# Holding back the first segment's expert gathers until the second segment's front has ended

## The chip, the core and the metric

The kernel runs on one core of a Trainium2 chip. The metric is the device time of one execution in microseconds (us). A core has five engines with an instruction queue each, worked off in order: TensorE (PE, with its weight loads listed apart as PEld), VectorE (DVE), ScalarE (ACT), GpSimd (POOL) and SyncE (SP, which here issues the plain DMAs). Engines wait for each other through semaphores. DMAs run beside the engines; indirect DMAs (gathers, one row of DRAM for each partition) are issued by POOL.

## The reference, cut to what matters

One layer: a mixer (four mLSTM heads and eight heads of forgetting attention), an output projection, and then a PEER channel mixer, which retrieves 8 x 16 experts out of 16384 for every token.

```python
def block(xb):                                   # 128 tokens
    qh = (xb @ w_query).reshape(tb, PEER_HEADS, 2, PEER_HALF)
    scores = einsum('thpc,hpnc->thpn', qh, keys)
    val, idx = top_k(scores, 16)                 # for each half of the key
    cand = val[..., 0, :, None] + val[..., 1, None, :]
    top_s, pos = top_k(cand.reshape(tb, 8, 256), 16)
    ids = take_along_axis(cand_id, pos)          # (tb, 128) experts per token
    gate = softmax(top_s)
    act = gelu(einsum('ted,td->te', u_emb[ids], xb))
    return einsum('te,ted->td', gate * act, v_emb[ids])
```

There are 1024 tokens of width 1024 (and 16 meta tokens before them); a row of `u_emb` or `v_emb` has 1024 float32 numbers.

## The kernel before, in words

The 1024 tokens are cut into four segments of two blocks of 128 (`SEGS`). Each segment goes through a front: `proj` (norm, projections, gates), `mlstm`, `fox` (attention) and `outp` (output projection, second norm, and at its end, line 854, the transposes of the normed tokens, 16 per segment). The loop over `i` near the end of the program merges the front of segment `i` with `proj` of segment `i + 1`, and with `topk`, the choice of experts: that of segment 0 is merged into `i = 1`, that of segments 1 and 2 into `i = 3`. Weights are split for the matmuls into a high part `wh` (cast on ACT, line 277) and a low part `wl` (subtraction on DVE, line 282, or on POOL, line 280).

The experts are computed in two ways. Segments 1 and 2 take the dense way: `gates` builds a table of gate weights for all 16384 experts (matmuls `gout`, line 1136, from one-hot tiles that DVE, ACT and POOL, line 1134, write), and the dense loop at the end of the program multiplies with all of `peer_u` (matmuls `du`, line 289) and all of `peer_v` (matmuls `vo`, line 1222), 1920 and 3072 of them.

Segments 0 and 3 take the gathered way, `gather_rows`. For a block A or B of 128 tokens there are 128 gathers of `peer_u` (line 325: retrieved expert r of every token, 128 rows of 4 KB, so 0.524 MB), each followed by its use: a product with the tokens, summed along the row, on DVE (line 334, 11 of 16) or on POOL with the sum on ACT (lines 331 and 332, 5 of 16). Then 128 gathers of `peer_v` (line 361: all experts of one token); four of these make a group for eight matmuls `po` (line 383). `gather_items` yields all u of block A, then in turn four v of A and four u of B, then all v of B. A use of v stands behind all uses of u of its block.

The gathers of segment 0 are written in the program after `topk` of the last segment (`GP0 = 5`), through a pool of four tiles (`GATH`); a scheduler that runs a timeline of its own at build time sorts each engine's instructions and puts the gathers, which come last and so have the lowest priority, where it sees an engine free from the moment the indices exist. The gathers of segment 3 are `Paced`: each waits for a matmul of the dense loop, 1.08 gathers for a beat, with twelve tiles (`GATH2`); they stand behind those of segment 0 in POOL's queue. The order of each engine is fixed at build time.

Of the kernel before, what the change touches and what calls it, by code (L numbers as in the profile page):

```python
# [19 lines left out]
P = 128  # L20
# [71 lines left out]
def _block_kernel(ctx, tc, nc, I, out, dbg):  # L92
# [27 lines left out]
    def bank(name):  # L120
        turn_b[0] += 1
        if extra is not None and turn_b[0] % XB == 0:
            return extra[:, turn_b[0] // XB % 2, :]
        return ps.tile([P, 512], F32, tag="bank", name=name, bufs=2)
# [9 lines left out]
    dve, act, pe, pool_e, sync = nc.vector, nc.scalar, nc.tensor, nc.gpsimd, nc.sync  # L134
# [6 lines left out]
    ident = identr.bitcast(F32)  # L141
# [67 lines left out]
    def rsqrt(o, x, scale, t):  # L209

        act.activation(o, x, AF.Ln, bias=epsc[0:x.shape[0]], scale=scale)
        act.activation(o, o, AF.Exp, scale=-0.5)
        act.activation(t, o, AF.Square)
        dve.scalar_tensor_tensor(t, x, EPS / scale, t, op0=OP.add, op1=OP.mult)
        dve.tensor_scalar(t, t, -0.5 * scale, 1.5, op0=OP.mult, op1=OP.add)
        dve.tensor_mul(o, o, t)
# [32 lines left out]
    def rawt(name):  # L249
        return wp.tile([P, L], F32, tag="raw", name=name, bufs=RAW)  # L250
# [5 lines left out]
    for i in range(3):  # L256
        c = slice(i * 512, min(L, i * 512 + 512))
        for e, t in enumerate((oz, zo)):
            t = t[0:NH_F, 0:c.stop - c.start]
# [134 lines left out]
    def gather_items(S, share, gp):  # L394

        A, B = (gather_rows(gp, S, lb, share) for lb in range(NB))
        yield from A.u
        for i in range(0, P, 4):
            yield from A.v[i:i + 4]
            yield from B.u[i:i + 4]  # L400
        yield from B.v


    def segment(sg):
        S = SimpleNamespace()
        S.sg = sg
        S.idT = None
        S.nb = nb = SEGS[sg]
        S.xb0 = xb0 = sum(SEGS[:sg])
        S.off = off = NMETA if sg == 0 else 0  # L410
        S.nx = nb * P
        S.n = S.nx + off
        S.c0 = 0 if sg == 0 else NMETA + xb0 * P
        S.chunks = ([(0, NMETA)] if sg == 0 else []) + [(off + i * P, P) for i in range(nb)]
        S.hx = len(S.chunks) - nb
        S.xs = slice(xb0 * P, xb0 * P + S.nx)
        S.T1 = S.c0 + S.n
        return S

    def tok_proj(wsrc, xh, xl, tbs, consume):  # L420

        bks = [acc_bank("tk") for _ in tbs]
        for kp in range(4):
            if xl is None:
                raw = rawt("raw")[:, 0:1024]
                sync.dma_start(raw, wsrc[kp])
                for k in (2 * kp, 2 * kp + 1):
                    for b, (ti, (s0, w)) in zip(bks, tbs):
                        pe.matmul(b[0:w, :], xh[:, k, s0:s0 + w], raw[:, k % 2 * 512:(k % 2 + 1) * 512],
                                  start=(k == 0), stop=(k == KT - 1))  # L430
                continue
            for kk, (h, l) in enumerate(halves(wsrc[kp], 2, share=SHARE)):
                k = 2 * kp + kk
                for b, (ti, (s0, w)) in zip(bks, tbs):
                    a, c = xh[:, k, s0:s0 + w], xl[:, k, s0:s0 + w]
                    for i, (x, wx) in enumerate(((a, h), (a, l), (c, h))):
                        pe.matmul(b[0:w, :], x, wx, start=(k == 0 and i == 0), stop=(k == KT - 1 and i == 2))
        for b, (ti, (s0, w)) in zip(bks, tbs):
            consume(ti, w, b)
# [376 lines left out]
    def outp(S):  # L816

        nb, xb0, yh, yl = S.nb, S.xb0, S.yh, S.yl
        if dbg: dbg("yh", S.sg, yh); dbg("yl", S.sg, yl)
        h2p = sp.tile([P, NB, D], F32, tag="u0", name="h2b")  # L820
        h2s = [h2p[:, b, :] for b in range(nb)]
        for b in range(nb):
            sync.dma_start(h2s[b], I["x"][(xb0 + b) * P:(xb0 + b + 1) * P, :])
        for nq in range(2):
            def take_w(ti, w, b):
                o = h2s[ti][:, nq * 512:(nq + 1) * 512]
                dve.tensor_add(o, o, b)
            tok_proj(I["wo"][nq], yh, yl, [(b, (b * P, P)) for b in range(nb)], take_w)
            yield
        gffn = rawt("gffn")[:, 0:D]  # L830
        sync.dma_start(gffn, I["g_ffn"].partition_broadcast(P))
        if S.sg <= DENSE[1]:
            half_ = slice((S.sg - DENSE[0]) % 2 * NX, ((S.sg - DENSE[0]) % 2 + 1) * NX)
            xh, xl = Xh[:, :, half_], Xl[:, :, half_]
        else:
            xh = hp.tile([P, KT, NTOK], F32R, tag="hh", name="xh3")[:, :, 0:nb * P]
            xl = hp.tile([P, KT, NTOK], F32R, tag="hl", name="xl3")[:, :, 0:nb * P]
        if S.sg in Q32:
            xh, xl = xh.bitcast(F32), None
        S.xh, S.xl = xh, xl  # L840
        for b in range(nb):
            gb_ = xb0 + b
            sync.dma_start(h2d[gb_ * P:(gb_ + 1) * P, :], h2s[b])
            xn = rawt("xn")[:, 0:D]
            ssq = sp.tile([P, 3], F32, tag="ssq", name="ssq")
            act.activation(xn, h2s[b], AF.Square, accum_out=ssq[:, 0:1])
            rsqrt(ssq[:, 1:2], ssq[:, 0:1], 1.0 / D, ssq[:, 2:3])
            dve.scalar_tensor_tensor(xn, h2s[b], ssq[:, 1:2], gffn, op0=OP.mult, op1=OP.mult)
            if S.sg not in DENSE:
                sync.dma_start(xnd[gb_ * P:(gb_ + 1) * P, :], xn)  # L850
            for half in range(2):
                tb = bank("xT")
                for i in range(4):
                    pe.transpose(tb[:, i * P:(i + 1) * P], xn[:, (4 * half + i) * P:(4 * half + i + 1) * P], ident)
                dsth = xh[:, 4 * half:4 * half + 4, b * P:(b + 1) * P]
                if xl is not None:
                    dstl = xl[:, 4 * half:4 * half + 4, b * P:(b + 1) * P]
                tbv = tb.rearrange("p (k t) -> p k t", k=4)
                act.copy(dsth, tbv)
                if xl is not None:  # L860
                    dve.tensor_sub(dstl, tbv, dsth.bitcast(F32))
        yield
# [111 lines left out]
    segs = [segment(i) for i in range(len(SEGS))]  # L974
    NPROJ, NTOP = 2 + 1 + 8 + 2 + 8, NH_P

    def main(S):
        yield from fox(S)
        yield from outp(S)
# [19 lines left out]
            yield  # L999

    def gather(S, share, gp):
        for ask, use in gather_items(S, share, gp):
            use(ask()[0])

    class Paced:

# [18 lines left out]
        def use(self):  # L1025
            _, f, t = self.open.pop(0)
            with ExitStack() as es:
                for k in ("pe", "dve"):
                    if k in seen:
                        es.enter_context(tc.issue_after(seen[k].ins))  # L1030
                f(t)
# [11 lines left out]
    def gather_first(at):  # L1043
        if GP0 == at:
            gather(segs[0], GS0, gp)


    for i in range(-1, len(SEGS)):
# [9 lines left out]
        if i >= 0:  # L1058
            S = segs[i]
# [227 lines left out]
```

## Time and profile before

| | |
|---|---|
| median of 3 runs | 3746.05 us (3735.21 to 3759.56) |
| profiled execution | 3742.05 us, span 3740.3 us |
| PE / DVE / POOL / ACT busy | 81% / 69% / 52% / 38% of the span |
| granted TensorE clock, mean | 0.890 of full speed |
| HBM read, written | 860.91 MB, 67.47 MB |

"Busy" counts an engine's instructions without waits. A wait is told as "idle before, and what ended it". The granted clock is a share of full speed, 1.0 being 2.4 GHz and 0.5 being 1.2 GHz. Each `po` matmul stands in the trace as two records (2048 for 1024).

### The profile page before, as it was taken

To read this page: it belongs to the slowest core of one execution; us is meant where nothing else is said; L and a number is where in the kernel's file an instruction comes from. 1 tells how busy PE (TensorE), PEld (TensorE's weight loads), DVE (VectorE), ACT (ScalarE), POOL (GpSimd) and SP (SyncE) were. 2 spreads that over 40 slices of the span, in tenths; PEclk is the share of its full clock that TensorE was granted. 3 is DMA by queue.
4 is the path that set the end of the run, shared out by engine and by line. 5 is a ranking of instruction groups with operands and counts; after the bars stand their busy time and mean duration, and the time that the engine had idled before them with its cause. 6 is when DMAs were issued, how large, how long until landed. Compare 5 with 4: busy or idle time off the path is not lost. (4 is left out here: it accounts for less than half of the span.)

```text
span 3740.3 us, 47105 instructions
## 1 busy us (share of the span) xinstructions
PE 3040.7 (81%) x15233; PEld 2324.6 (62%) x15233; DVE 2581.1 (69%) x6272; ACT 1435.7 (38%) x2915; POOL 1944.4 (52%) x1575
## 2 busy tenths in 40 slices
PE   7798776657778889887886599865798888989999
PEld 6686666446556667656765476644576555666667
DVE  6566999987447988888997443877655656654434
ACT  4565443345343323335655432322333332332222
POOL 3121566666545545557656422888655555543430
PEclk9899876768788999988998899887899999999999
DMA  4455577777877778767776777988888788889983
GB/s 140 123 156 166 191 228 243 240 226 250 229 241 238 242 223 257 240 239 263 271 251 234 272 253 248 325 285 287 283 295 293 269 284 290 313 317 328 330 292 109
DMA packets 375899, 931.54 MB, mean 249 GB/s; under 512 B 59316, under 2 KB 145556, under 8 KB 373604
## 3 DMA queue, kind: packets, MB, share of 16 engines
q0 software_dynamic: 161216, 552.56, 44.3%
q1 hardware_dynamic: 214436, 375.97, 30.4%
q8 instruction: 120, 1.97, 0.2%
q14 instruction: 127, 1.04, 0.1%
HBM read 860.91 MB, written 67.47 MB: 248 GB/s over the span
## 5 line engine op out<-in xcount | busy, mean ns | idle before, releaser
L282 DVE TENSOR_TENSOR wl<-raw,wh 128x512 fp32r<-128x512 f32 x736 | 608.4, 833 | 508.6 <-ACT wh L277 455.7
L277 ACT CAST wh<-raw 128x512 fp32r<-128x512 f32 x896 | 543.0, 617 | 971.4 <-DMA raw<-in_peer_v 208.5
L325 POOL DMA_INDIRECT gu<-in_peer_u,idx x512 | 578.9, 1131 | 567.9 <-PE po L383 173.7
L361 POOL DMA_INDIRECT gv<-in_peer_v,idT x512 | 558.2, 1090 | 603.4 <-PE po L383 198.2
L334 DVE SCALAR_TENSOR_TENSOR gu<-gu,xng 128x1024 f32<-128x1024 f32 x352 | 512.8, 1467 | 99.0 <-DMA gu<-in_peer_u,idx 91.9
L1222 PE MATMUL vo<-wh,Wh 128*128 128x512 f32 x1024 | 395.1, 418 | 138.5 <-ACT wh L277 114.0
L1222 PE MATMUL vo<-wl,Wh 128*128 128x512 f32 x1024 | 423.1, 413 | 12.2 <-DVE wl L282 12.1
L331 POOL TENSOR_TENSOR gu<-gu,xng 128x1024 f32<-128x1024 f32 x160 | 389.7, 2436 | 71.8 <-DMA gu<-in_peer_u,idx 66.3
L1222 PE MATMUL vo<-wh,Wl 128*128 128x512 f32 x1024 | 415.8, 408 | 0.0
L280 POOL TENSOR_TENSOR wl<-raw,wh 128x512 fp32r<-128x512 f32 x160 | 217.8, 1361 | 325.9 <-ACT wh L277 294.7
L1222 PEld LDWEIGHTS vo<-wh,Wh 128*128 128x128 f32 x1024 | 198.4, 197 | 231.9 <-ACT wh L277 136.3
L383 PE MATMUL po<-gv,Z 128*32 128x512 f32 x2048 | 273.4, 641 | 78.0 <-DMA gv<-in_peer_v,idT 78.0
L332 ACT ACTIVATE gu<-gu 128x1024 f32<-128x1024 f32 x160 | 169.2, 1058 | 364.6 <-POOL gu L331 357.2
L289 PE MATMUL du<-xh,wh 128*128 128x512 f32 x640 | 259.0, 405 | 30.3 <-ACT wh L277 30.3
L289 PE MATMUL du<-xh,wl 128*128 128x512 f32 x640 | 258.8, 405 | 22.2 <-DVE wl L282 22.1
L289 PE MATMUL du<-xl,wh 128*128 128x512 f32 x640 | 256.2, 400 | 0.0
L1222 PEld LDWEIGHTS vo<-wl,Wh 128*128 128x128 f32 x1024 | 204.0, 199 | 69.9 <-DVE wl L282 19.8
L1222 PEld LDWEIGHTS vo<-wh,Wl 128*128 128x128 f32 x1024 | 203.3, 199 | 51.9 <-issue 6.7
L1136 PE MATMUL gout<-A,B 128*128 128x128 f32 x1024 | 161.3, 310 | 65.1 <-POOL B L1134 51.9
L1136 PEld LDWEIGHTS gout<-A,B 128*128 128x128 f32 x1024 | 146.6, 217 | 93.8 <-POOL B L1134 69.9
L1227 DVE TENSOR_TENSOR acc<-acc,vo 128x512 f32<-128x512 f32 x256 | 164.7, 680 | 47.2 <-PE vo L1222 46.7
L1207 DVE TENSOR_TENSOR Wl<-w,Wh 128x512 fp32r<-128x512 f32 x128 | 96.0, 754 | 133.2 <-ACT Wh L1206 113.5
(431 smaller groups left out, 6696.3 us busy)
## 6 DMA issues: line engine op xcount, KB each, us to landing
raw<-in_ut SPq DMA_DIRECT2D x128, 512.0 KB
raw<-in_peer_v SPq DMA_DIRECT2D x256, 256.0 KB
raw<-in_wf SPq DMA_DIRECT2D x64, 512.0 KB
gd<-G SPq DMA_DIRECT2D x16, 2048.0 KB
Gt<-gd SPq DMA_DIRECT2D x32, 1024.0 KB
raw<-in_wt SPq DMA_DIRECT2D x48, 512.0 KB
raw<-in_wq SPq DMA_DIRECT2D x48, 512.0 KB
raw<-in_wo SPq DMA_DIRECT2D x32, 512.0 KB
```

The lines of the kernel that those rows point to most:

```text
L277: act.copy(h, part)
L280: pool_e.tensor_sub(l, part, h.bitcast(F32))
L282: seen["dve"] = dve.tensor_sub(l, part, h.bitcast(F32))
L289: seen["pe"] = pe.matmul(o, w, x[:, c], start=(first and i == 0), stop=(last and i == 2))
L325: d = pool_e.indirect_dma_start(out=t, out_offset=None, in_=I["peer_u"], in_offset=bass.IndirectOffsetOnAxis(ap=S.idx[:, lb, r:r + 1], axi ...
L331: pool_e.tensor_tensor(t, t, xn[0], op=OP.mult)
L332: act.activation(t, t, AF.Copy, accum_out=G.actv[:, r:r + 1])
L334: dve.scalar_tensor_tensor(t, t, 1.0, xn[0], op0=OP.mult, op1=OP.mult, accum_out=G.actv[:, r:r + 1])
L361: d = pool_e.indirect_dma_start(out=t, out_offset=None, in_=I["peer_v"], in_offset=bass.IndirectOffsetOnAxis(ap=S.idT[lb][:, tok:tok + 1], ...
L383: last = pe.matmul(G.po[32 * q_:32 * q_ + 32, n, :], z[:, q_, 31 - j:63 - j], rows[q_][:, n * 512:(n + 1) * 512], start=(j == 0), stop=(j ...
L1136: pe.matmul(bk[:, u * P:(u + 1) * P], B[:, u, :], A[:, u, :], start=True, stop=True)
L1222: seen["pe"] = pe.matmul(bks[b], w[:, cw], v, start=(ii == 0 and i == 0), stop=(ii == GRP - 1 and i == 2))
```

## The change

`S.done` keeps the last transpose of a segment's `outp`. In `gather`, which only segment 0 uses, the first gather gets a dependency on `segs[1].done`, and every later gather is put behind the first one in POOL's order. Nothing is added to any engine but this wait, and no instruction is taken away; the scheduler sorts all engines anew.

```diff
@@ outp
-                    pe.transpose(tb[:, i * P:(i + 1) * P], xn[:, (4 * half + i) * P:(4 * half + i + 1) * P], ident)
+                    S.done = pe.transpose(tb[:, i * P:(i + 1) * P], xn[:, (4 * half + i) * P:(4 * half + i + 1) * P], ident)
@@ gather
     def gather(S, share, gp):
+        first = None
         for ask, use in gather_items(S, share, gp):
-            use(ask()[0])
+            with tc.issue_after(first.ins) if first else nullcontext():
+                t, d = ask()
+            if first is None:
+                first = d
+
+                tc.add_manual_dep(d.ins, segs[1].done.ins.name, mybir.DependencyInfo(
+                    mybir.DependencyClass.Sync, mybir.DependencyReason.DATA), reason="hold")
+            use(t)
```

Three places in the new order. The first is POOL while segment 1's attention runs (`kqa` are the loads of keys and queries for a head; with 528 columns those of segment 1, with 784 those of segment 2). Before, the first gathers stand behind the second head of segment 1:

```order
L729 DMA kqa<-kd 66x2x528
L731 DMA kqa<-qd 66x2x256
L280 TENSOR_TENSOR wl<-raw,wh 128x512 x2
L325 DMA gu<-in_peer_u,idx 128x1024 x4
L280 TENSOR_TENSOR wl<-raw,wh 128x512
L331 TENSOR_TENSOR gu<-gu,xng 128x1024
L325 DMA gu<-in_peer_u,idx 128x1024
```

Now they stand behind the second head load of segment 2:

```order
L280 TENSOR_TENSOR wl<-raw,wh 128x512 x5
L729 DMA kqa<-kd 66x2x784
L731 DMA kqa<-qd 66x2x256
L280 TENSOR_TENSOR wl<-raw,wh 128x512 x6
L729 DMA kqa<-kd 66x2x784
L731 DMA kqa<-qd 66x2x256
L325 DMA gu<-in_peer_u,idx 128x1024 x6
L331 TENSOR_TENSOR gu<-gu,xng 128x1024
```

DVE's order moves the same way: of segment 0's 176 products of line 334, 67 stood ahead of the last write of `xl` (the copy of those transposes) of segment 1, 45 more up to that of segment 2, 54 more up to that of segment 3 and 10 in `gates`; now it is 0, 72, 63 and 41.

The second place is POOL at the end of `gates`. Before, the last one-hot tile is followed by 56 gathers of v and then segment 3's gathers:

```order
L1134 TENSOR_SCALAR B<-iota,jT,gT 128x128 x9
L361 DMA gv<-in_peer_v,idT 128x1024 x4
L1134 TENSOR_SCALAR B<-iota,jT,gT 128x128 x6
L361 DMA gv<-in_peer_v,idT 128x1024 x56
L325 DMA gu<-in_peer_u,idx 128x1024 x13
```

Now by four u and 128 v, and gathers of u with their products stand among the last one-hot tiles:

```order
L331 TENSOR_TENSOR gu<-gu,xng 128x1024
L1142 TENSOR_SCALAR B<-iota,jT,gT 128x128
L361 DMA gv<-in_peer_v,idT 128x1024 x2
L325 DMA gu<-in_peer_u,idx 128x1024 x4
L361 DMA gv<-in_peer_v,idT 128x1024
L331 TENSOR_TENSOR gu<-gu,xng 128x1024
L361 DMA gv<-in_peer_v,idT 128x1024 x127
L325 DMA gu<-in_peer_u,idx 128x1024 x14
```

So PE passes the last group of segment 0's v behind 1721 of the 4992 matmuls of the dense loop, where it was 707, and the first group of segment 3's behind 2388, where it was 1440. From segment 3's last block of v on, the two orders agree again (3660 and 3673).

The third place is ACT in the middle of the dense loop, where segment 3's sums of line 332 stand among the casts. Before, two of them are this far apart:

```order
L332 ACTIVATE gu,actv<-gu 128x1024
L1206 CAST Wh<-w 128x512 x2
L277 CAST wh<-raw 128x512 x2
L1206 CAST Wh<-w 128x512
L277 CAST wh<-raw 128x512
L1206 CAST Wh<-w 128x512
L277 CAST wh<-raw 128x512
L1155 ACTIVATE w<-w 128x512
L277 CAST wh<-raw 128x512
L1158 ACTIVATE w<-du 128x512
L332 ACTIVATE gu,actv<-gu 128x1024
```

Now there are four in a stretch of that length:

```order
L332 ACTIVATE gu,actv<-gu 128x1024
L1163 ACTIVATE w<-w 128x512
L1166 ACTIVATE w<-du 128x512
L277 CAST wh<-raw 128x512 x2
L332 ACTIVATE gu,actv<-gu 128x1024
L277 CAST wh<-raw 128x512 x2
L1214 CAST Wh<-w 128x512
L332 ACTIVATE gu,actv<-gu 128x1024
L277 CAST wh<-raw 128x512
L332 ACTIVATE gu,actv<-gu 128x1024
```

## Rows read from the trace of the kernel before

**Rows 1.** Busy time by stretch of the span (us), each engine with its count of records, then granted clock, DMA share and GB/s; the stretches are segment 1's front, segment 2's, segment 3's, `gates`, and four stretches of the dense loop: up to the last gather of segment 0, segment 3's first block of u, the mixed v and u, and the last block of v to the end.

```profile
380.00:763.00 383.00, 264.30 (x1376) 230.06 (x1376) 376.98 (x973) 161.10 (x346) 246.50 (x176) 0.75 0.72 227
763.00:1140.00 377.00, 265.89 (x1348) 205.47 (x1347) 239.87 (x450) 158.74 (x359) 214.89 (x170) 0.77 0.78 237
1140.00:1690.00 550.00, 477.53 (x2359) 357.41 (x2357) 464.87 (x1616) 180.22 (x374) 290.90 (x232) 0.93 0.75 241
1690.00:2115.00 425.00, 335.63 (x2133) 267.87 (x2133) 352.27 (x1252) 246.21 (x505) 283.50 (x247) 0.90 0.69 248
2115.00:2330.00 215.00, 186.04 (x895) 133.82 (x891) 84.92 (x143) 58.16 (x99) 55.45 (x56) 0.94 0.81 270
2330.00:2625.00 295.00, 197.90 (x710) 147.52 (x710) 224.42 (x280) 87.67 (x159) 251.90 (x168) 0.83 0.86 295
2625.00:3335.00 710.00, 608.67 (x2701) 440.93 (x2700) 426.68 (x640) 222.84 (x390) 392.18 (x303) 0.94 0.84 294
3335.00:3740.00 405.00, 390.62 (x1922) 277.01 (x1921) 173.23 (x299) 108.38 (x185) 122.11 (x122) 0.98 0.76 267
```

**Rows 2.** Timeline of PE at the transposes that end a front (start, duration, instruction, idle before it): segment 1's, the last ones of segment 2's and of segment 3's.

```profile
763.08 1.06 PE L854 MATMUL extra<-identr,xn 128*128 128x128 f32 x4
...
1132.06 1.12 PE L854 MATMUL xT<-identr,xn 128*128 128x128 f32 x4 [1.43 <-DVE xl L861]
...
1686.90 1.97 PE L854 MATMUL xT<-identr,xn 128*128 128x128 f32 x8 [3.07 <-DVE xl L861]
```

**Rows 3.** Groups of DVE by line: the first two rows from 380 to 763, the third from 763 to 862 (busy us, mean ns of one, then idle before).

```profile
L334 DVE SCALAR_TENSOR_TENSOR gu<-gu,xng 128x1024 f32<-128x1024 f32 x66 | 97.8, 1483 | 3.6 <-DMA gu<-in_peer_u,idx 3.6
L282 DVE TENSOR_TENSOR wl<-raw,wh 128x512 fp32r<-128x512 f32 x67 | 68.2, 1023 | 1.4 <-ACT wh L277 1.4
...
L282 DVE TENSOR_TENSOR wl<-raw,wh 128x512 fp32r<-128x512 f32 x8 | 5.4, 670 | 0.0
```

**Rows 4.** The products of line 334 in the three stages after that: 763 to 1140, 1140 to 1690, 1690 to 2115.

```profile
L334 DVE SCALAR_TENSOR_TENSOR gu<-gu,xng 128x1024 f32<-128x1024 f32 x48 | 66.9, 1402 | 33.7 <-DMA gu<-in_peer_u,idx 33.6
...
L334 DVE SCALAR_TENSOR_TENSOR gu<-gu,xng 128x1024 f32<-128x1024 f32 x54 | 75.0, 1390 | 38.1 <-DMA gu<-in_peer_u,idx 31.3 <-issue 6.8
...
L334 DVE SCALAR_TENSOR_TENSOR gu<-gu,xng 128x1024 f32<-128x1024 f32 x10 | 14.8, 1483 | 10.0 <-DMA gu<-in_peer_u,idx 10.0
```

**Rows 5.** Busy time by stretch of line 383 alone (PE, PEld, clock, DMA share, GB/s).

```profile
763.00:1140.00 377.00, 21.57 (x144) 4.26 (x144) 0.77 0.78 237
1140.00:1690.00 550.00, 50.17 (x320) 9.65 (x320) 0.93 0.75 241
1690.00:2115.00 425.00, 50.21 (x336) 9.97 (x336) 0.90 0.69 248
...
2625.00:3335.00 710.00, 61.56 (x512) 13.36 (x512) 0.94 0.84 294
```

**Rows 6.** Groups by line in `gates`, 1690 to 2115: PE's matmuls of the table, POOL's one-hot tiles, POOL's gathers of v.

```profile
L1136 PE MATMUL gout<-A,B 128*128 128x128 f32 x1024 | 161.3, 310 | 65.1 <-POOL B L1134 51.9 <-DVE cid L923 4.3 <-DVE B L1134 2.5
...
L1134 POOL TENSOR_SCALAR B<-iota,jT,gT 128x128 f32<-128x128 f32 x128 | 141.5, 1108 | 66.9 <-PE gout L1136 51.6 <-ACT gT L1109 11.7 <-POOL B L1134 2.0
...
L361 POOL DMA_INDIRECT gv<-in_peer_v,idT x83 | 92.4, 1113 | 49.2 <-PE po L383 29.1 <-issue 10.9 <-PE gout L1136 4.0
```

**Rows 7.** Busy time of PE from 2150 to 2250, by line: 1222 (`vo`), 289 (`du`), 383 (`po`).

```profile
2150.00:2250.00 100.00, 43.29 (x184) 34.06 (x183) 1.00 0.77 254
...
2150.00:2250.00 100.00, 44.87 (x192) 35.80 (x192) 1.00 0.77 254
...
2150.00:2250.00 100.00, 13.46 (x112) 2.92 (x112) 1.00 0.77 254
```

**Rows 8.** Segment 3's first block of u, 2330 to 2625: the gathers as a group, and the longest wait.

```profile
L325 POOL DMA_INDIRECT gu<-in_peer_u,idx x128 | 158.8, 1241 | 48.2 <-issue 23.1 <-DVE gu L334 9.6 <-DMA raw<-in_peer_v 8.9
...
ACT gu L332 <- POOL gu L331: 149.0, 31, 9.2
```

**Rows 9.** The mixed stretch, 2625 to 3335: POOL's three groups by line, then PE's busy time of line 1222 and of line 289.

```profile
L361 POOL DMA_INDIRECT gv<-in_peer_v,idT x132 | 152.7, 1157 | 118.9 <-issue 29.2 <-PE vo L1222 27.9 <-ACT wh L277 20.2
L325 POOL DMA_INDIRECT gu<-in_peer_u,idx x128 | 136.4, 1066 | 164.9 <-PE vo L1222 76.2 <-PE du L289 42.7 <-issue 21.6
L331 POOL TENSOR_TENSOR gu<-gu,xng 128x1024 f32<-128x1024 f32 x43 | 104.5, 2432 | 27.9 <-DMA gu<-in_peer_u,idx 25.0 <-DVE wl L282 1.6 <-DVE w L1203 0.7
...
2625.00:3335.00 710.00, 364.01 (x1412) 277.01 (x1410) 0.94 0.84 294
...
2625.00:3335.00 710.00, 190.72 (x776) 150.38 (x777) 0.94 0.84 294
```

**Rows 10.** DMA in the mixed stretch: bytes in all, and those of the queue of the gathers (packets, MB, share of 16 engines).

```profile
DMA packets 92117, 208.56 MB, mean 294 GB/s; under 512 B 7245, under 2 KB 35917, under 8 KB 92076
...
q0 software_dynamic: 37560, 136.76, 53.9%
```

**Rows 11.** The stretch in which DMA moved most, by all engines as in rows 1: its best 50 us, and 200 us.

```profile
3350.00:3400.00 50.00, 50.00 (x270) 32.59 (x272) 21.41 (x41) 13.70 (x24) 24.90 (x25) 1.00 1.01 361
3350.00:3550.00 200.00, 200.00 (x1031) 134.87 (x1030) 90.00 (x162) 56.65 (x98) 82.79 (x84) 1.00 0.93 332
```

## The prediction

> **What bounds the kernel now.** I read the table of busy time by stretch first, because the kernel has stages with different limits [rows 1]. While segment 1's front runs (380 to 763 us), DVE is busy 377.0 of 383 us and PE only 264.3, at a granted clock of 0.75. That stage is DVE's. In segment 2's front nobody is full. In segment 3's front DVE (85%) and PE (87%) are both near it, and in `gates` DVE has 83%. In the dense loop PE leads, but in three manners: up to segment 0's last gather it is full almost all the time, then, in segment 3's first block of u, POOL is (251.9 of 295) and PE falls to 67%, then PE has 86% in the mixed stretch, and from 3335 on it is full again. The timeline of PE dates the ends of the fronts: 764, 1133 and 1689 us [rows 2]. So two things are to be priced: what segment 1's front gains when the gathers leave it, and what the dense loop pays for taking more of them.
>
> **The front of segment 1.** The change takes 67 products of line 334 off DVE before 763; they cost 97.8 us there [rows 3]. What is left for DVE is 377.0 - 97.8 = 279 us. If DVE stayed as full as now (98%), the stage would take 284 us, 99 less. But the gathers are the low-priority work that keeps it full. Segment 3's front shows what its leading engine reaches, 87% [rows 1]; with that the stage takes 321 us, 62 less. I take 80 less, in the middle. The wait itself costs nothing that I can find: behind the waiting gather on POOL stands work of segment 2's front only, which begins after the transposes that the gather waits for.
>
> A second effect may come on top. The subtraction of line 282 takes 1.023 us on average in this stage and 0.670 in the stretch behind it [rows 3], so 67 of them could give back 67 x 0.35 = 23 us when POOL is quieter. I leave that for the range, since the product of line 334 is as slow where the gathers go (1.40, 1.39 and 1.48 us, [rows 4]).
>
> The Trainium skill (SBUF — State Buffer, section "SBUF: two separate sides") says that VectorE with two SBUF inputs and a GpSimd instruction hold a shared port pair exclusively, and one blocks while the other runs. By that rule the 23 us are real in this stage, and the sum would be 23 us lower; but they would be paid again wherever the moved products meet POOL's.
>
> **The stages up to the dense loop.** Segment 2's front gets 72 products of line 334 for 45, so 27 x 1.40 = 38 us more on DVE [rows 4], which is busy 64% [rows 1], and loses its `po` matmuls, 21.6 us of PE [rows 5]. The ends are +38 and -22; most of it lies in idle time of DVE, so I take +5. Segment 3's front gets 9 more, 12.5 us on an engine that is 85% busy: I take +8 (ends 0 and +13, since PE has its 50.2 us of `po` still nearly whole). `gates` gets 41 for 10: 31 x 1.48 = 46 us of DVE, and on POOL some 14 products of line 331 at 2.43 us [rows 9], 34 us. POOL is what PE waits for there (51.9 us, [rows 6]). The ends are 0 and +80. DVE would go from 83% to 94% and POOL too gets fuller, so not all of it is hidden: +35. The dense loop then starts 80 - 5 - 8 - 35 = 32 us sooner, at about 2083.
>
> **The dense loop.** PE's order now has 1721 matmuls before segment 0's last group of v, where it had 707, and 18 groups of v more. When PE is full, a dense matmul takes (100 - 13.46) / 376 = 0.230 us [rows 7], and a group of v 61.56 / 32 = 1.92 us [rows 5]. So this part is 1014 x 0.230 + 18 x 1.92 = 268 us longer; nothing of it is lost, since PE is full in it. Each group now has about 14 us of PE work around it; four buffers managed a group in 15 us before (56 gathers in 215 us).
>
> Segment 3's first block of u is 128 gathers as before, and its order holds 667 matmuls for 733. POOL sets its length (251.9 busy of 295, [rows 1, 8]), so it stays 295 us: 0.
>
> The mixed stretch, 128 v and 128 u, held 2233 matmuls and now holds 1272. PE alone would need 1272 x 0.230 + 61.6 = 354 us. POOL needs more: its 392.2 us of work [rows 1] and 29.2 + 21.6 us of issue gaps [rows 9] are for 260 gathers, so 256 need 436 us. DMA needs more still: of 208.56 MB, 136.76 were gathers [rows 10], and 71.8 MB served 1412 + 776 = 2188 matmuls [rows 9], 32.8 KB each. Now 256 x 0.524 + 1272 x 0.0328 = 176 MB. At the rate of the best 50 us, 361 GB/s, this takes 487 us; at the 332 GB/s of the best 200 us, 530 [rows 11]; at today's mean of 294, 598. PE was full in the fast rows, so DMA was not what held the kernel there, and I take a value near the best row, 500 us: 710 - 500 = 210 less. The ends are 436 and 598.
>
> The last stretch has 13 matmuls fewer, -3. The dense loop as a whole is 268 - 210 - 3 = 55 us longer.
>
> **Sum.** 3742 (the profiled execution, 2 us around its span; the median of the runs is 4 above it) - 80 + 5 + 8 + 35 + 268 - 210 - 3 = **3765 us**, 0.5% above the median. What is gained in the front is spent in the dense loop, where segment 3's gathers start about 236 us later and have to be done at the same matmul as before.
>
> **The rivals.** A change of this kernel under 1% (37 us: below 3709 or above 3783) can't be told from none.
>
> *Near cancellation*, the forecast: chance 0.40, its own range 3709 to 3790.
>
> *Slower: the mixed stretch is DMA's.* For it: DMA already has a share of 0.84 there and of 0.86 in the block of u, and ACT's order now has its sums of line 332 twice as close, each of which can hold the casts behind it (149.0 us of waits of that kind in the block of u, [rows 8]). Against it: 361 GB/s was reached with PE full. At 530 to 598 us the time is 3795 to 3863. It decides from 518 us on, that is below 340 GB/s. Chance 0.27.
>
> *The front gains nothing*: segment 1's front hangs on a chain, at a low clock, and not on DVE's load. For it: nothing but the 0.75 clock and PE's 69%. Against it: DVE idles 6 us in 383. Then 80 us are missing: 3845. Chance 0.08.
>
> *Faster: DMA keeps up and the front gains in full.* The mixed stretch then goes down to POOL's 436 us, which alone gives 3701; with segment 1's front 99 + 23 shorter as well, 3659. For it: the order asks for more in flight, and there are twelve buffers. It decides from 444 us on. Chance 0.25.
>
> The Trainium skill (DMA: Bandwidth & Descriptors, section "Bandwidth") gives 425 GB/s for one large transfer of a core whose neighbour idles. By that figure the 176 MB would take an estimated 414 us, under POOL's 436, and the sum would be 3701; no row of this case holds more than 361 for 50 us.
>
> **Range and chances.** The range is 3685 to 3845: it takes in the upper part of the faster case and all of the slower one but the slowest DMA, and leaves out about a tenth on each side. Faster 0.25, within 1% 0.40, slower 0.27 + 0.08 = 0.35.
>
> **What would show it.** In the changed profile no gather should stand before segment 1's transposes, and these should come at about 684 us instead of 763, with DVE well below 98% before them and PE's clock above 0.75; those of segment 3 should come at about 1620; the first `vo` at about 2083; segment 0's last gather at about 2570, with PE full from the start of the loop to there; then 295 us of u and 500 us of mixed work at 350 GB/s or more. If DMA stays near 300 GB/s in the mixed stretch, the kernel is slower and this step failed. If `gates` takes much more than 460 us, POOL was dearer there than I priced it. If segment 1's front ends after 740, DVE was not what held it.

## The result, and the profile after

The changed kernel takes 3787.69 us (median of 4 runs, 3777.27 to 3800.34); the kernel before took 3740.63 beside it (4 runs). The ratio is 1.0122, with a 95% interval of 1.0089 to 1.0156: 1.2% slower, on the far side of the 1% that I had called no change. The profiled execution took 3778.46 us, 36 more than that of before.

First the table of busy time by stretch of the changed kernel, cut at its own stage boundaries (columns as in [rows 1]): segment 1's front, segment 2's, segment 3's, `gates`, the dense loop up to segment 0's last gather, segment 3's first block of u, the mixed stretch, the rest.

```profile
380.00:629.00 249.00, 218.12 (x1389) 195.74 (x1390) 236.75 (x856) 130.67 (x288) 59.76 (x48) 0.93 0.51 143
629.00:990.00 361.00, 246.48 (x1193) 201.59 (x1193) 290.63 (x481) 167.21 (x379) 262.64 (x188) 0.78 0.82 251
990.00:1544.00 554.00, 481.36 (x2340) 361.05 (x2340) 483.25 (x1642) 188.71 (x389) 304.75 (x239) 0.93 0.77 246
1544.00:2010.00 466.00, 344.26 (x1996) 284.42 (x1995) 409.57 (x1288) 255.98 (x520) 340.69 (x275) 0.83 0.66 235
2010.00:2519.00 509.00, 462.50 (x2229) 332.36 (x2228) 201.67 (x340) 139.07 (x233) 136.60 (x134) 0.95 0.75 251
2519.00:2833.00 314.00, 197.02 (x649) 145.08 (x645) 223.11 (x290) 88.73 (x161) 256.07 (x171) 0.78 0.85 290
2833.00:3350.00 517.00, 391.12 (x1713) 261.81 (x1713) 288.52 (x445) 139.47 (x251) 374.04 (x294) 0.88 0.92 333
3350.00:3777.00 427.00, 400.46 (x1941) 283.49 (x1941) 185.72 (x316) 114.54 (x196) 127.98 (x128) 0.98 0.76 266
```

Against [rows 1] segment 1's front lost 134 us, the next two -16 and +4, `gates` +41: the gates end 105 us sooner. From there on the stages change by +294, +19, -193 and +22: the mixed stretch is shorter, and the dense loop as a whole is 142 us longer.

The groups of DVE by line in segment 1's front, which answer to [rows 3]:

```profile
L282 DVE TENSOR_TENSOR wl<-raw,wh 128x512 fp32r<-128x512 f32 x67 | 50.8, 759 | 3.7 <-ACT wh L277 3.6
```

The product of line 334 is gone, and the same 67 subtractions take 759 ns each, where they took 1023.

`gates` by line, 1544 to 2010, beside [rows 6] (lines above 1000 are 8 higher in the changed kernel):

```profile
L1144 PE MATMUL gout<-A,B 128*128 128x128 f32 x1023 | 185.6, 340 | 113.0 <-POOL B L1142 74.0 <-DVE A L1134 18.8 <-DVE B L1142 7.8
...
L1142 POOL TENSOR_SCALAR B<-iota,jT,gT 128x128 f32<-128x128 f32 x128 | 149.3, 1171 | 62.5 <-PE gout L1144 47.6 <-ACT gT L1117 7.1 <-PE q L289 3.4
```

PE's idle time before `gout` grew from 65.1 to 113.0 us; the largest part, 74.0, is again put down to POOL's B.

POOL by line in the next stretch, 2010 to 2519:

```profile
L361 POOL DMA_INDIRECT gv<-in_peer_v,idT x129 | 130.5, 1012 | 346.9 <-PE po L383 299.7 <-issue 25.6 <-DVE gu L334 15.8
```

For 299.7 of 509 us POOL stands before a gather of segment 0 until a `po` matmul gives one of its four tiles back. Segment 3's gathers are behind it in the queue. So the engine that the next block needs for 256 of 314 us is 27% busy here (136.60 of 509).

Last PE's matmuls into `vo`: first the page of before, then the page of the changed kernel, then its block of u (2519 to 2833) and its mixed stretch (2833 to 3350), each with the sums on ACT:

```profile
L1222 PE MATMUL vo<-wh,Wh 128*128 128x512 f32 x1024 | 395.1, 418 | 138.5 <-ACT wh L277 114.0
...
L1230 PE MATMUL vo<-wh,Wh 128*128 128x512 f32 x1024 | 387.0, 428 | 222.0 <-ACT wh L277 171.2
...
L1230 PE MATMUL vo<-wh,Wh 128*128 128x512 f32 x140 | 54.4, 492 | 84.0 <-ACT wh L277 70.9 <-DVE acc L1235 12.9 <-issue 0.2
L332 ACT ACTIVATE gu<-gu 128x1024 f32<-128x1024 f32 x38 | 40.2, 1058 | 159.4 <-POOL gu L331 159.4
...
L1230 PE MATMUL vo<-wh,Wh 128*128 128x512 f32 x272 | 94.8, 455 | 94.0 <-ACT wh L277 90.1 <-DVE acc L1235 1.4 <-issue 1.3
L332 ACT ACTIVATE gu<-gu 128x1024 f32<-128x1024 f32 x40 | 42.3, 1057 | 211.6 <-POOL gu L331 211.6
```

PE's idle time before these matmuls rose from 138.5 to 222.0 us. In the mixed stretch PE waits 90 us for ACT's casts, and ACT, which works in order, waits 212 us for POOL's products; before, these were 56 and 93 us in a stretch of 710. I had priced that stretch by DMA.

### The profile page after: what moved, and what is told of

Its sections match the earlier page's. It is cut to its first block, busy times and chain, and to the rows that moved or that the text cites. A ratio compares the mean times of both kernels' runs of the same rounds, so it can differ in the third digit from the quotient of the medians.

```text
span 3776.7 us, 47132 instructions
## 1 busy us (share of the span) xinstructions
PE 3059.5 (81%) x15233; PEld 2333.6 (62%) x15233; DVE 2554.8 (68%) x6272; ACT 1435.0 (38%) x2911; POOL 1949.5 (52%) x1575
## 5 line engine op out<-in xcount | busy, mean ns | idle before, releaser
L282 DVE TENSOR_TENSOR wl<-raw,wh 128x512 fp32r<-128x512 f32 x736 | 570.1, 781 | 513.5 <-ACT wh L277 484.8
L361 POOL DMA_INDIRECT gv<-in_peer_v,idT x512 | 543.6, 1062 | 665.4 <-PE po L383 319.3
L1230 PE MATMUL vo<-wh,Wh 128*128 128x512 f32 x1024 | 387.0, 428 | 222.0 <-ACT wh L277 171.2
L1230 PE MATMUL vo<-wh,Wl 128*128 128x512 f32 x1024 | 424.4, 417 | 0.0
L1144 PE MATMUL gout<-A,B 128*128 128x128 f32 x1024 | 185.8, 340 | 113.0 <-POOL B L1142 74.0
L1144 PEld LDWEIGHTS gout<-A,B 128*128 128x128 f32 x1024 | 165.3, 242 | 142.4 <-POOL B L1142 94.8
L1215 DVE TENSOR_TENSOR Wl<-w,Wh 128x512 fp32r<-128x512 f32 x128 | 103.9, 814 | 156.9 <-ACT Wh L1214 113.6
```

Of the source, the lines that this page charges most:

```text
L282: seen["dve"] = dve.tensor_sub(l, part, h.bitcast(F32))
L361: d = pool_e.indirect_dma_start(out=t, out_offset=None, in_=I["peer_v"], in_offset=bass.IndirectOffsetOnAxis(ap=S.idT[lb][:, tok:tok + 1], ...
L1144: pe.matmul(bk[:, u * P:(u + 1) * P], B[:, u, :], A[:, u, :], start=True, stop=True)
L1230: seen["pe"] = pe.matmul(bks[b], w[:, cw], v, start=(ii == 0 and i == 0), stop=(ii == GRP - 1 and i == 2))
```

## The experiments

The theory at the outset: segment 0's tail is what the dense loop pays for, since segment 3's gathers start when it ends. The rival: the moved gathers are only work that falls due later.

**Segment 0's last v cut, with the hold and without.**

```diff
-        yield from B.v
+        yield from (B.v if S.sg else B.v[:4] + B.v[-4:])
```

> The changed kernel with the last v block of segment 0 cut from 32 groups to 2 (so the PEER output of 120 of that block's 128 tokens is left out). Theory (the front's gain of about 105 us at the end of gates is real, and it is lost in the dense loop because segment 0's v delay segment 3's gathers by some 290 us): without that tail segment 3 starts with the dense loop, the dense loop falls from 1767 to about 1550 us, and the time is about 3560, some 100 us below the same cut made in the kernel before. Rival (the dense loop is as long as PE and DMA need, wherever segment 3's gathers start): only the 30 groups' own PE work goes, 58 us, so about 3720 and no more than 40 us below the same cut in the kernel before.

> The kernel before with the same cut (30 of the 32 groups of segment 0's last v block left out); its dense loop has the same order of instructions as the cut changed kernel. Theory: the tail of 215 us goes and segment 3 starts with the dense loop, whose length becomes that of the cut changed kernel within 1%, about 1550 us; gates end near 2100, so about 3660. Rival: 27 to 58 us less than the kernel before, 3680 to 3715, with a dense loop that differs from that of the cut changed kernel.

Measured: 3592.25 us (ratio to before 0.9599, 0.9571 to 0.9628) with the hold, 3594.35 (0.9606, 0.9568 to 0.9644) without. Neither theory had that: the cut is worth 195 us with the hold and 146 without, and the two kernels come out the same. The gathers of u (line 325) and of v (line 361) from 380 to 2330 in the kernel with the hold, and then in the one without (count, duration, first and last start):

```profile
L325 POOL DMA_INDIRECT gu<-in_peer_u,idx x340: 935/972/3173, 632.7 to 2322.0; - x170
...
L361 POOL DMA_INDIRECT gv<-in_peer_v,idT x136: 936/1032/2885, 1051.2 to 2088.7; - x136
```

```profile
L325 POOL DMA_INDIRECT gu<-in_peer_u,idx x340: 937/976/3165, 380.7 to 2327.3; - x170
...
L361 POOL DMA_INDIRECT gv<-in_peer_v,idT x136: 934/1025/2186, 861.0 to 1842.9; - x136
```

The hold starts the gathers 252 us later, and at 2330 us both kernels have sent equally many. Segment 3's front ends 150 us sooner with the hold, the gates 75 us sooner, and at 2330 hardly any lead is left: from there to the end PE has 5217 matmuls with the hold and 5249 without. So what the front gains is paid again between 1545 and 2330 us, as the rival says, even without the tail; and the tail is worth far more than its 30 groups of 1.92 us [rows 5], 58 us, as the theory says. The cut also takes 120 gathers of 0.524 MB, 63 MB, off DMA, so it doesn't tell a wait for tiles from plain traffic; the runs that follow leave all gathers in.

**Own tiles for segment 3's gathers**, so that they need not wait for segment 0's memory.

```diff
-GATH2 = 12
+GATH2 = 10
...
+    gp = pool("gather", GATH)
     mid = ctx.enter_context(ExitStack())
     front = ctx.enter_context(ExitStack())
-    gp = pool("gather", GATH, mid)
```

> The changed kernel with the four gather tiles of segment 0 in a place of their own, so that segment 3's gather tiles no longer lie over them and needn't wait for segment 0's last v (and ten tiles for segment 3 in place of twelve, for want of room). All work is done. Theory (segment 3's gathers are late because their tiles are the same memory as segment 0's): segment 3's first u block runs beside segment 0's last v, where POOL is busy 27% and DVE 40%; the 314 us in which PE is at 63% mostly go, and the time is 3640 to 3710. Rival (the dense loop is bound by the sum of DMA and PE work): within 1% of the changed kernel, 3750 to 3810.

> The kernel before with the same two edits (own place for segment 0's gather tiles, ten tiles for segment 3). Theory: there the tail is only 215 us, so segment 3 starts some 200 us sooner at most; between 3670 and 3740, and slower than the changed kernel with these edits. Rival: within 1% of the kernel before.

Measured: 3694.29 (0.988, 0.9858 to 0.9902) with the hold, 3715.31 (0.9923, 0.9896 to 0.9949) without it. Both lie within what the theory said. The second one lies within its rival too (within 1% of before), so only the first decides between them. The table of busy time of the kernel with the hold, 2066 (its first `vo`) on:

```profile
2066.00:2500.00 434.00, 354.93 (x1505) 257.38 (x1505) 285.45 (x412) 136.98 (x246) 304.59 (x223) 0.89 0.87 307
2500.00:2750.00 250.00, 240.55 (x1137) 173.23 (x1138) 109.17 (x184) 67.71 (x118) 63.31 (x64) 0.97 0.72 239
```

POOL now works 304.6 of the first 434 us, on segment 3's u beside segment 0's v, at 307 GB/s where the changed kernel had 251.

**The control: ten tiles, in the old place.**

```diff
-GATH2 = 12
+GATH2 = 10
```

> The changed kernel with ten tiles for segment 3's gathers in place of twelve, lying where they lay (over segment 0's). It is the control of the run with own tiles, which had ten as well. If that run's gain came from the place (segment 3's gathers no longer wait for segment 0's memory): no gain here, 3775 to 3815 us, and segment 3's first gather still behind segment 0's last, at about 2510. Rival: the gain came from fewer gathers in flight (less of DMA taken from the weights): 3690 to 3730 here too.

Measured: 3733.08 us (0.9968, 0.9938 to 0.9997), between the two expectations. Segment 3's first gather still starts at 2518, so the place is as before, and yet 55 us are gone; own tiles are worth 39 more. In the page PE's wait before `vo` fell:

```profile
L1230 PE MATMUL vo<-wh,Wh 128*128 128x512 f32 x1024 | 373.3, 426 | 169.4 <-ACT wh L277 132.0
```

It is 169.4 us for 222.0: 53 us less, where the medians differ by 55 and the profiled executions by 41. Why two tiles fewer let the casts come sooner is not settled. The order at build time differs as well: the mixed stretch of this run lasts from 2830 to 3410 and holds 2041 of PE's matmuls, for 1713 in the changed kernel, so the same gathers are spread over more of the loop; no run here changes that order alone. Every edit has all engines sorted anew, so part of a difference between any two of these runs may come from the order. Ten tiles in the old place without the hold were not tried.

**Fewer of segment 3's products on POOL.**

```diff
-GS3 = (2, 5, 8, 11, 14)
+GS3 = (2, 8, 14)
```

> The changed kernel with 3 of 16 products of segment 3's u on POOL in place of 5: 32 products of 2.43 us (78 us) fewer on POOL, 32 of about 1.45 (46 us) more on DVE, half of them in the first block of u. If that block is POOL's (256 busy of 314 us) and PE's waits for the casts come from sums on ACT that wait for POOL's products: the block falls from 314 to 270 to 295, PE's idle time before vo by 40 or more from 222 us, 3725 to 3765. Rival: the block is DMA's (0.85, 290 GB/s): it stays at 305 to 320, 3775 to 3805. The mixed stretch (333 GB/s, 0.92 of DMA) should stay at 505 to 525 by either.

Measured: 3747.8 us (1.0009, 0.9981 to 1.0036), 40 less than the changed kernel, as the theory had it.

```profile
2515.00:2790.00 275.00, 169.90 (x590) 124.10 (x589) 201.57 (x291) 65.75 (x118) 204.72 (x144) 0.79 0.89 303
2790.00:3320.00 530.00, 410.11 (x1793) 272.24 (x1792) 322.50 (x517) 132.59 (x235) 363.12 (x293) 0.89 0.94 347
```

The block of u fell from 314 to 275 us, so POOL set its length. PE's wait before `vo` fell to 194.6 us, by 27 and not by 40 or more. The mixed stretch took 530 us, not 505 to 525, with 1793 of PE's matmuls in it for 1713. It moved 347 GB/s for 333: DMA had room there that the changed kernel did not use.

**`gates` without POOL.**

```diff
-GPOOL = 1
+GPOOL = 0
```

> The changed kernel with all 512 of the one-hot tiles B of the stage of gates on DVE; 128 of them stood on POOL, behind gathers and products. If PE's wait there (74 us for POOL's B) is what the held-back gathers made longer, and POOL's queue its reason: gates falls from 466 us to 410 to 440, and the time to 3735 to 3765. Rival: DVE is the limit of this stage already (409.6 busy of 466), and 128 tiles of 0.40 us more make 461: gates stays at 460 to 490, the time at 3775 to 3810.

Measured: 3797.3 us (1.014, 1.0093 to 1.0186): the rival. The table for `gates` (1544 to 2026) and its groups by line:

```profile
1544.00:2026.00 482.00, 350.31 (x2032) 286.26 (x2024) 439.91 (x1429) 261.95 (x529) 206.54 (x157) 0.82 0.68 239
```

```profile
L1144 PE MATMUL gout<-A,B 128*128 128x128 f32 x1024 | 186.1, 335 | 99.7 <-DVE B L1142 73.9 <-ACT G L1146 17.8 <-ACT A L1138 3.7
L1142 DVE TENSOR_SCALAR B<-iota,jT,gT 128x128 f32<-128x128 f32 x512 | 178.6, 410 | 0.0
```

With nothing of B on POOL, PE waits the same 74 us, for DVE. So the row that names POOL in [rows 6] names the engine that came last, and taking its work away gained nothing. DVE is busy 91% of `gates` here, and 88% in the changed kernel.

**The kernel before, with segment 0's products off POOL.**

```diff
-GS0 = (2, 5, 8, 11, 14)
+GS0 = ()
```

> The kernel before with all products of segment 0's u on DVE and none on POOL. In segment 1's front DVE gets some 30 products of about 1.45 us more, POOL loses 30 of 2.45. The question is what makes DVE's other work slow there (the subtraction of line 282: 1.023 us on average, 0.759 once the gathers are gone). If it is POOL's products, the mean falls to 0.85 or less although DVE has more to do, and segment 1's front grows by less than 25 us from 383. Rival: it is the gathers themselves, their issue on POOL or the rows that they write: the mean stays at 0.95 or more, and the front takes 400 to 430 us. Time 3740 to 3790 by the first, 3760 to 3820 by the second.

Measured: 3692.07 us in one run, 49 below before, and below what either theory allowed. DVE by line from 380 to 744, where segment 1's transposes begin (the last one comes at 757, for 763 in [rows 2]):

```profile
L334 DVE SCALAR_TENSOR_TENSOR gu<-gu,xng 128x1024 f32<-128x1024 f32 x103 | 133.6, 1302 | 14.8 <-DMA gu<-in_peer_u,idx 14.8
L282 DVE TENSOR_TENSOR wl<-raw,wh 128x512 fp32r<-128x512 f32 x66 | 51.6, 787 | 2.4 <-ACT wh L277 2.4
```

The gathers are still there, and 37 products more stand on DVE, and yet the front is shorter; only POOL's products are gone, and line 282 falls from 1023 to 787 ns and line 334 from 1483 to 1302. So it is POOL's products that slow DVE, for the most part: at most the last 28 ns, from 787 to the 759 of the changed kernel, where neither products nor gathers are, can be the gathers'.

**Both causes together.** The same line in the changed kernel, then with own tiles as well, with the hold and without:

```diff
-GS0 = (2, 5, 8, 11, 14)
+GS0 = ()
```

> The changed kernel with all products of segment 0's u on DVE, none on POOL: with the run of the kernel before without POOL's products (3692) it shows what the hold costs when the two engines no longer slow each other. If the hold's loss is the late start of segment 3's gathers (their tiles lie on segment 0's): slower than that run by 25 to 70 us, 3715 to 3760, with segment 0's last gather after 2450. Rival: the hold lost because the moved products meet POOL's in later stages: then nothing is lost now, 3640 to 3700. The mean of the product of line 334 should be about 1.30 us for 1.45 to 1.52 in the changed kernel's second and third fronts by either.

> The changed kernel with own tiles for segment 3's gathers (ten) and all products of segment 0's u on DVE. If the two are separate causes (memory that comes free late; two engines that slow each other): their gains add, 3694 - 49 = 3645, 3620 to 3665. Rival: with own tiles DVE is full in the fronts and in gates, and 80 products more on it take back what POOL's quiet gives: 3675 to 3710.

> The same two edits in the kernel before, without the hold. The hold by itself, with both causes out of the way, is worth the difference to the run with the hold: if the front's gain is kept when nothing waits for segment 0's memory, this one is slower by 10 to 50 us, 3640 to 3690 (additive: 3715 - 49 = 3666). Rival: most of the hold's gain in the front was the quiet of POOL, which this kernel has anyway: within 10 us of the run with the hold or faster.

Measured: 3720.74 (0.9959, 0.9932 to 0.9987), 3621.72 (0.9701, 0.966 to 0.9742) and 3650.72 (0.9779, 0.9733 to 0.9826). All three as the theory of two separate causes had them in time; in the first, line 334 took 1287 and 1330 ns in the second and third fronts, for 1450 and 1523; only segment 0's last gather comes before 2433 there, not after 2450. The products on DVE were worth 67, 73 and 65 us in these three pairs. Laid side by side, the hold costs or gives this; the last two columns are read from the profiled executions, at the first `vo`:

| | without hold | with hold | the hold | dense loop starts sooner by | and lasts longer by |
|---|---|---|---|---|---|
| as they were | 3740.63 | 3787.69 | +47 | 90 | 126 |
| segment 0's products on DVE | 3692.07 (one run) | 3720.74 | +29 | 78 | 110 |
| its last v cut | 3594.35 | 3592.25 | -2 | 57 | 53 |
| own tiles, ten | 3715.31 | 3694.29 | -21 | 133 | 97 |
| own tiles, ten, and products on DVE | 3650.72 | 3621.72 | -29 | 101 | 66 |

In the last two rows the intervals of the ratios overlap by a hair (0.9896 and 0.9902; 0.9733 and 0.9742), though the slowest run with the hold is faster than the fastest without it in both (3700.12 and 3705.61; 3632.5 and 3644.5), so the gain is likely but not beyond doubt. What agrees in both: where segment 3's gathers need not wait for segment 0's, the hold no longer costs anything. The last two columns show why both first theories had a part of it: in every pair the loop starts sooner and lasts longer, so the held work does fall due later; with shared tiles and all gathers it takes back more than the lead, with own tiles two thirds to three quarters of it. In the kernel before, own tiles also put the first `vo` 58 us later (2199.7 for 2141.6), for a reason that stays open, and part of the lead of 133 is that. These rows have ten tiles, too, and how much of the turn is the place and how much the number they don't split; the run with ten tiles in the old place says 39 and 55 us with the hold.

**Segment 3's products off POOL as well.**

```diff
-GS3 = (2, 5, 8, 11, 14)
+GS3 = ()
```

> As the run with the hold, own tiles and segment 0's products on DVE (3622), with segment 3's products on DVE as well: 80 products of 2.45 us fewer on POOL in the dense loop and 80 sums of 1.05 us fewer on ACT, 80 products of some 1.3 us (104 us) more on DVE, which is busy about 60% there. If POOL's products and the sums behind them still hold the casts back: 3580 to 3610, PE's idle time before vo down by 30 us or more. Rival: with own tiles the dense loop is PE's and DMA's (320 GB/s from 2600 to 3000): no change, 3610 to 3635.

Measured: 3556.09 us (0.9508, 0.9471 to 0.9545), 66 below the run it starts from and more than expected; it beats both kernels, by 4.9% and 6.1%. PE's wait before `vo` in the page of the run it starts from, and in its own:

```profile
L1230 PE MATMUL vo<-wh,Wh 128*128 128x512 f32 x1024 | 383.6, 415 | 97.3 <-ACT wh L277 85.8
...
L1230 PE MATMUL vo<-wh,Wh 128*128 128x512 f32 x1024 | 376.5, 409 | 74.0 <-ACT wh L277 51.9
```

And its table of busy time where the dense loop begins:

```profile
2050.00:2330.00 280.00, 259.28 (x1195) 189.12 (x1190) 206.91 (x357) 74.54 (x131) 164.39 (x142) 0.97 1.01 369
```

The wait is 74.0 us, 23 less and not the 30 or more that I had expected. Of the 71 us between the two profiled executions 49 lie behind the first `vo` (1485 us for 1534): PE is idle 32 us less there, which is about what its waits for casts lost (23 before `vo` and 12 before `du`), and busy 17 us less, at a granted clock of 0.97 for 0.96. The other 22 lie ahead of the first `vo`, for a reason that stays open. DVE has more to do in the loop and yet is not busier: 239 products of line 334 for 164, at 1220 ns each for 1324, its subtractions at 687 ns for 806, and 874 us busy for 888. In the first 280 us of the loop DMA moves 369 GB/s and PE is 93% busy.

## Why the prediction was right in its range and wrong in its sum

The range (3685 to 3845) held the time, and the forecast of 3765 was 23 us low. The case I held likeliest, near cancellation, holds the time in its own range (3709 to 3790), but the loss is just over the 1% (3783) that I had called no change. That the sum came so near is in part luck: the front gained 54 us more and the dense loop lost 87 us more than I had put down, and these two errors stand against each other:

| term | predicted | measured |
|---|---|---|
| segment 1's front | -80 | -134 |
| segment 2's, segment 3's | +5, +8 | -16, +4 |
| `gates` | +35 | +41 |
| up to segment 0's last gather | +268 | +294 |
| block of u | 0 | +19 |
| mixed stretch | -210 | -193 |
| last stretch | -3 | +22 |

*The front.* The way was right: DVE held this stage, and with the products gone it lasts 249 us. I had left two things small. DVE stayed 95% busy (236.75 of 249) where I took a share between 87 and 98%. And 377.0 - 97.8 - 236.75 = 42 us left DVE beside the products' 97.8: 5 of them are the reads of the accumulator that go with each product, 17 the subtractions of line 282, and the rest many other instructions that took less time. I had 23, for line 282 alone, and kept them out of the sum. At 95% those 42 us are 45 of the 54 that were missing.

For that effect I had cited the Trainium skill (SBUF — State Buffer, section "SBUF: two separate sides"). The run of before without POOL's products shows that most of the slowing is POOL's products, which agrees with it. What I said would follow, that it is paid again wherever the moved products meet POOL's, holds too: in the second and third fronts of the changed kernel the product of line 334 takes 1450 and 1523 ns for 1402 and 1390 [rows 4].

*`gates`.* +35 for +41 is right in size and wrong in its reason. I read POOL as the engine with no room; with B moved from POOL to DVE, the stage got 16 us longer (482 for 466). So room on POOL was not what it lacked, and DVE's is the likelier limit; how the 41 us divide between my 46 of DVE and 34 of POOL no run shows.

*The dense loop*, +55 forecast and +142 measured, is the step that failed. The table of busy time from the first `vo` on, before and then changed:

```profile
2141.00:3740.00 1599.00, 1379.72 (x6204) 998.68 (x6204) 908.12 (x1358) 472.95 (x827) 814.07 (x640) 0.93 0.82 283
...
2052.00:3777.00 1725.00, 1446.91 (x6509) 1021.84 (x6509) 894.02 (x1383) 474.74 (x830) 884.75 (x717) 0.91 0.82 285
```

PE's busy time grew by 67 us and its idle time by 59 (278 for 219); the rest stands ahead of it, where 42 us lie between the last `gout` and the first `vo`, for 29 before. Of the 67, 28 are the same matmuls into `vo` and `du`, which took 1277.5 us for 1249.2 at a granted clock of 0.91 for 0.93; the others are mostly the groups of segment 0's v that moved in, which the forecast had. What it did not have is most of the idle time, and the clock.

Three sentences of the prediction fail. "Nothing of it is lost, since PE is full in it": PE was full (458 of 467 us from the first `vo` to 2519), but POOL stood 300 us before tiles of segment 0 while segment 3's gathers waited behind it. Ten tiles in a place of their own took back 93 us: 39 against ten in the old place, and 55 by the number, for a reason that stays open. "DMA needs more still": the mixed stretch ran at 333 GB/s for 517 us, near the 500 I took, but DMA had room left: with fewer products on POOL it moved 347 GB/s there, and 369 in the first 280 us of the last run's loop. What PE waited for there were the casts behind ACT's sums, 90 us, and the sums waited for POOL's products. With all products off POOL and tiles of their own, the waits for casts fell by 35 us and the time by 66; but with two of five products off POOL the stretch still took 530 us, so its length is not explained to the end. And the block of u at 295: it took 314, and 275 with fewer products on POOL, so it was POOL's, as I had said; but POOL's waits before the gathers, which I had left as they were, grew from 48.2 to 64.1 us, 10 of these 16 behind products of DVE.

In the last stretch, +22 for -3, PE is idle 27 us for 14, and 8 of these 12 stand before `vo` (15.3 us for 7.4); the rest is more of its work behind the boundary at 3350.

*The rivals.* The slower one, the mixed stretch as DMA's, was to decide from 518 us on: it came to 517 and did not decide; its remark on ACT's sums, which stand twice as close and can each hold the casts behind them, was the part that came true: PE's waits for casts in the mixed stretch rose from 56 to 90 us before `vo`. The front that gains nothing is excluded by the 134 us. Of the faster one, the front gained more than in full (134 us for 99 + 23), but the mixed stretch was far from POOL's 436.

I had cited 425 GB/s from the Trainium skill (DMA: Bandwidth & Descriptors, section "Bandwidth"); the 369 of the last run is the highest that a stretch read here holds.

## What to carry to other kernels

When work is held back, ask which queue and which memory it takes with it: here the held gathers delayed others that stood behind them in POOL's order and over their tiles, and the hold cost 47 us with shared tiles and nothing with separate ones, of which there were ten and not twelve. Two engines that both have room can still cost each other: moving POOL's share of a product to DVE, which is the busier one, gained 49 us in one run and 65 to 73 in three pairs for segment 0's products, and 66 for segment 3's. And a wait put down to an engine doesn't say that this engine is the limit; move its work away and see whether the wait moves to another name.

## What the runs showed of the hardware

The slowing of DVE beside POOL is not spread over all of its instructions. The rows of lines 334 and 282 of the changed kernel in its block of u, 2519 to 2833: first line 334 as a group (busy us, mean ns), then minimum, median and maximum ns of each:

```profile
L334 DVE SCALAR_TENSOR_TENSOR gu<-gu,xng 128x1024 f32<-128x1024 f32 x85 | 132.3, 1583 | 0.0
...
L334 DVE SCALAR_TENSOR_TENSOR gu<-gu,xng x85: 1208/1218/3886, 2537.9 to 2825.0; 128x1024 f32<-128x1024 f32 x85
...
L282 DVE TENSOR_TENSOR wl<-raw,wh x50: 676/686/3287, 2524.1 to 2824.4; 128x512 fp32r<-128x512 f32 x50
...
L331 POOL TENSOR_TENSOR gu<-gu,xng x38: 2346/2404/2717, 2551.7 to 2829.5; 128x1024 f32<-128x1024 f32 x38
```

The same lines in the last run, from 2100 to 3335, with no product on POOL:

```profile
L334 DVE SCALAR_TENSOR_TENSOR gu<-gu,xng x232: 1206/1218/1285, 2098.9 to 3133.1; 128x1024 f32<-128x1024 f32 x116
...
L282 DVE TENSOR_TENSOR wl<-raw,wh x342: 674/684/752, 2100.7 to 3333.3; 128x512 fp32r<-128x512 f32 x171
```

The medians are within 2 ns of each other. Beside POOL's products some DVE instructions take up to 2.67 and 2.60 us more, about one whole product of POOL (2.35 to 2.72); without them none takes more than 0.07 us over the median, although POOL sends 532 gathers in that stretch. So at least half of the instructions are not disturbed, the worst are held for about the length of the other engine's, and the gathers do not do it. The Trainium skill (SBUF — State Buffer, section "SBUF: two separate sides") states just that, an exclusive lock and not a split of bandwidth. A mean of 1583 ns hides it, the maximum shows it.
